# One PSUM pool, half-size weight tiles, and the seven-product form in four of eight pairs of k-tiles

## The chip, the cores and the metric

The kernel runs on one core of one Trainium2 chip. The metric is the time of the whole program on the device, in microseconds (us). Five engines with instruction streams of their own take part: TensorE (PE in the views; PEld is its weight load), VectorE (DVE), ScalarE (ACT), GpSimd (POOL) and SyncE (SP), which here only issues transfers. An engine runs its stream strictly in order; an instruction that has to wait for another engine or for a transfer holds up all that stand behind it on its own engine.

## What is computed

A transformer block on 256 tokens of width 2048: three token mixers run beside each other on the normalised input, their results are merged by gates and projected, and a SwiGLU layer follows. Cut to its large products:

```python
h = rms_norm(x, g_mix)
proj = h @ w_in                                # 2048 -> q/k/v of the mixers and 3 x 2048 gates
...                                            # attention of the mixers gives oa, ob, oc
merged = gate0 * (oa @ w_br_a) + gate1 * (ob @ w_br_b) + gate2 * (oc @ w_br_c)
x = x + merged @ w_o                           # 2048 x 2048
hf = rms_norm(x, g_ffn) @ w_ffn_in             # 2048 -> 2 x 5632
x = x + (silu(hf[:, :5632]) * hf[:, 5632:]) @ w_ffn_out
```

Everything is fp32. Weights are read once, so each goes through the core as it comes from memory.

## The kernel before

**Precision.** A product of fp32 numbers is made of three products of reduced-width numbers. `split` (line 83) writes `hi`, a rounded copy of a tile, by ScalarE (line 86) and `lo = source - hi` by VectorE (line 87). Each product then takes three matmuls into one PSUM bank: hi x hi, hi x lo, lo x hi (lines 183 to 185, or 548 to 550 in the FFN).

**Tiles.** The 256 tokens are two tiles of 128 rows (`T` = 2), the 2048 input channels 16 k-tiles of 128, and outputs come in blocks of 512 columns, one PSUM bank each. `product` (line 161) makes one block of 512 columns for both token tiles. It loads weights through `load` (line 150) in tiles `raw` of 4 k-tiles (1 MB, three buffers), and splits them two k-tiles at a time into `whi` and `wlo` (four buffers each, so a tile takes over the buffer of the tile four before it; `raw` tiles turn in the same way). Weight loads are issued by SP.

**Stages.** In order: keys and values of the memory tokens; the input projection, with the attention work as side jobs between its steps (`tick`, line 140); gates and branch products with the merge (lines 456 to 479); the output projection with the residual and the transposes of the new `x` (lines 482 to 495); the FFN (from line 502).

**FFN.** The 5632 hidden columns are 11 chunks of 512; each chunk takes 512 columns of the half under Silu (A) and the same 512 of the other half (B). `in_seven` (line 525) computes a chunk. It sees two neighbouring k-tiles, the two token tiles and A, B as a 2 x 2 by 2 x 2 block product. In 5 of the 8 pairs of k-tiles it makes the eight block products plainly (steps `d3` to `d7`: 24 matmuls each). In the other three (`s0` to `s2`) it makes seven products (21 matmuls) from sums of blocks: the sums of activations are made once (`stationary_forms`, tiles `fh`, `fl`), the sums of weights by VectorE for each chunk (lines 583, 584, 588, 589; `t2`, `t3`, `t4` hold them), and the steps `6`, `7` and `4` at the end of the list run over the sums of all three. `ORDER` lists the steps of a chunk. The results stand in six banks `mmX`, `mmY`, `mmZ`, `mmW`, `mmV`, `mmQ`; X is copied out twice while it is still summing. At the end of a chunk ScalarE and VectorE combine the banks in `SA` and `SB` (lines 609 to 614), ScalarE takes Silu (623), VectorE multiplies (624), and TensorE transposes the result with the identity (line 229, tiles `tp`) for the second FFN product, which runs after chunks 4, 8 and 11 over the chunks made since. `r_f`, the scale of the second norm for each token, is applied in Silu and in the multiply.

**PSUM.** There are eight banks. Up to the output projection four belong to a pool "mm" (accumulators) and four to a pool "at" (transposes, attention); ahead of the FFN both are closed and opened again with seven and one (lines 503 to 505). The transposes of a chunk thus share one bank.

**Order.** The instruction streams are laid down when the program is built: a scheduler puts each engine's ready instructions in the order of its own estimate of time, with the order of the program text as priority and buffers as limits. What an engine executes next is therefore fixed; which instructions stand beside each other on an engine can only be read from the streams.

Of the kernel before, what the change touches and what calls it, by code (L numbers as in the profile page):

```python
# [18 lines left out]
P = 128  # L19
# [6 lines left out]
NC = 512  # L26
KF = DFF // P
PK, LOAD = 2, 4
# [23 lines left out]
SEVEN = 3  # L52
ORDER = "s0 d3 s1 d4 s2 d5 6 d6 7 d7 4".split()
ORDER0 = "d3 d4 d5 s0 s1 d6 s2 6 d7 7 4".split()
# [3 lines left out]
def encoder_block(ctx: ExitStack, tc: tile.TileContext, a: dict, out: bass.AP):  # L58
# [7 lines left out]
    banks = ExitStack()  # L66
    pools = {"mm": banks.enter_context(tc.tile_pool(name="pmm", bufs=4, space=bass.MemoryType.PSUM)),
             "at": banks.enter_context(tc.tile_pool(name="pat", bufs=4, space=bass.MemoryType.PSUM))}
# [7 lines left out]
    def at_bank(name):  # L76
        return pools["at"].tile([P, NC], F32, name=name, tag="at")

    def mm_bank(name="mm"):
        return pools["mm"].tile([P, NC], F32, name=name, tag="mm")  # L80
# [69 lines left out]
    def load(src, k0, nk):  # L150

        raw = wp.tile([P, LOAD, NC], F32, name="raw")
        if nk % PK:
            c = k0 % PK * NC
            nc.sync.dma_start(out=raw[:, 0], in_=src[k0 // PK][:, c:c + NC])
        else:
            nc.sync.dma_start(out=raw[:, :nk].rearrange("p (u k) n -> p u (k n)", k=PK),
                              in_=src[k0 // PK:(k0 + nk) // PK].rearrange("u p n -> p u n"))
        return raw

    def product(src, lhs, nk, head=(), beside={}):


        ps = [mm_bank() for _ in range(T)]
        k0 = 0
        while k0 < nk:
            n = head[0] if head else min(LOAD, nk - k0)
# [5 lines left out]
            for b in range(0, n, PK):  # L173
                m = min(PK, n - b)
                hi = wp.tile([P, PK, NC], F32R, name="whi", bufs=4)
                lo = wp.tile([P, PK, NC], F32R, name="wlo", bufs=4)
                split(hi[:, :m], lo[:, :m], raw[:, b:b + m])
                for i in range(m):
                    k = k0 + b + i
                    xh, xl = lhs(k)  # L180
                    for t in range(T):
                        c = slice(t * P, (t + 1) * P)
                        nc.tensor.matmul(ps[t], lhsT=xh[:, c], rhs=hi[:, i], start=(k == 0), stop=False)  # L183
# [182 lines left out]
    def attend(qs, ks, vs, bias, kt):  # L366
# [36 lines left out]
        def turn(i):  # L403
# [7 lines left out]
            pTs.append(pT)  # L411

        turn(0)
        ops = at_bank("o")
        for i in range(g):
            yield PV_LAG
            if i + 1 < g:
# [301 lines left out]
```

## Time and profile before

| | |
|---|---|
| median of three timed runs | 1429.48 us (1427.87 to 1429.51) |
| profiled execution | 1432.02 us |
| its span, first to last instruction | 1430.2 us |
| mean granted TensorE clock | 0.994 |
| moved by DMA | 276.99 MB, mean 194 GB/s |

The profiled execution is 2.5 us above the median, and 1.8 us of it lie outside the span. In the rows below, a busy time stands with its share of the span and, after an x, with a count; a group's row gives line, engine, operation, result <- operands, then total busy time and mean nanoseconds of one, then the idle time of that engine just before these instructions with what ended most of it. Matmuls overlap in TensorE's pipeline, so the mean of one (393 ns for `mm<-whi,xT`) is more than the spacing from one to the next. VectorE's splits of weights (`wlo<-raw,whi`, 497 of them) are its largest group with 612.6 us; ScalarE's copies for them (`whi<-raw`) take 524.0 us.

### The profile page before, as it was taken

Reading aid. Unit: us, or ns where it says so; the run is one execution under the profiler, and the core shown is the slowest. Engines: PE = TensorE matmul, PEld = TensorE weight load, DVE = VectorE, ACT = ScalarE, POOL = GpSimd, SP = SyncE. Lnnn points to the kernel's source line nnn. Section 1 sums busy time; section 2 is a strip of 40 time slices with the busy share of each in tenths; the row PEclk is TensorE's granted clock in tenths of the full one; section 3 lists DMA queues with packets and bytes.
Section 4 is the critical chain, followed back from the end, with each engine's and each line's share of the span. In section 5 each row is a group of like instructions: output and inputs, shape, how many; then the busy total and the mean of one; then the engine's idle time right before and its main releaser. Section 6 shows DMA issues by size and latency. Waiting matters only on the chain.

```text
span 1430.2 us, 16503 instructions
## 1 busy us (share of the span) xinstructions
PE 1400.4 (98%) x6323; PEld 1151.6 (81%) x6323; DVE 963.3 (67%) x1191; ACT 741.0 (52%) x971; POOL 78.8 (6%) x146
## 2 busy tenths in 40 slices
PE   6999999999999999999899999999999999999998
PEld 4778788888888888888687788888888888888887
DVE  5666776754455555555688987557988855788763
ACT  5576556544444444444456555435655643456542
POOL 0012642200000000000000000000000000000000
PEclk8999999999999999999999999999999999999999
DMA  8876445456555555655455554555554555655562
GB/s 293 272 255 187 147 175 176 135 218 217 195 180 202 191 169 188 213 181 179 174 177 180 211 186 188 187 195 206 201 186 176 203 206 190 222 176 178 206 223 101
DMA packets 64510, 276.99 MB, mean 194 GB/s; under 512 B 5232, under 2 KB 7792, under 8 KB 52912
## 3 DMA queue, kind: packets, MB, share of 16 engines
q1 hardware_dynamic: 61984, 271.73, 54.8%
q10 hardware_dynamic: 2448, 4.22, 0.9%
q8 instruction: 49, 0.80, 0.2%
q14 instruction: 29, 0.24, 0.0%
HBM read 273.05 MB, written 2.88 MB: 193 GB/s over the span
## 4 chain that ended last, share of the span: by engine, by line
PE 89%; DMA 4%; POOL 2%; DVE 2%; ACT 2%; issue 1%; SPq 0%; ACTq 0%; DVEq 0%; POOLq 0%
PE mm L184 18%; PE mm L183 18%; PE mm L185 18%; PE mmY L549 2%; PE mmY L550 2%; PE mmY L548 2%; PE mmZ L549 2%; PE mmZ L550 2%; PE mmZ L548 2%; PE mmV L549 2%; PE mmV L550 2%; PE mmV L548 2%; PE mmQ L550 2%; PE mmQ L549 2%; PE mmQ L548 2%; PE mmX L549 1%
## 5 line engine op out<-in xcount | busy, mean ns | idle before, releaser
L87 DVE TENSOR_TENSOR wlo<-raw,whi 128x1024 fp32r<-128x1024 f32 (+1 forms) x497 | 612.6, 1238 | 393.4 <-ACT whi L86 392.1
L86 ACT ACTIVATE whi<-raw 128x1024 fp32r<-128x1024 f32 (+1 forms) x497 | 524.0, 1061 | 573.5 <-PE mm L185 367.1
L183 PE MATMUL mm<-whi,xT 128*128 128x512 f32 x640 | 250.6, 393 | 1.4 <-ACT whi L86 1.1
L184 PE MATMUL mm<-wlo,xT 128*128 128x512 f32 x640 | 250.2, 391 | 1.1 <-DVE wlo L87 1.1
L185 PE MATMUL mm<-whi,xT 128*128 128x512 f32 x640 | 249.5, 391 | 0.0
L183 PEld LDWEIGHTS mm<-whi,xT 128*128 128x128 f32 x640 | 120.1, 188 | 26.7 <-ACT whi L86 1.6
L184 PEld LDWEIGHTS mm<-wlo,xT 128*128 128x128 f32 x640 | 120.2, 188 | 26.3 <-DVE wlo L87 1.5
L185 PEld LDWEIGHTS mm<-whi,xT 128*128 128x128 f32 x640 | 120.2, 188 | 24.6
L184 PE MATMUL mm<-wlo,hT 128*128 128x512 f32 x352 | 138.0, 393 | 0.0
L185 PE MATMUL mm<-whi,hT 128*128 128x512 f32 x352 | 137.6, 393 | 0.0
L183 PE MATMUL mm<-whi,hT 128*128 128x512 f32 x352 | 134.9, 391 | 0.0
L184 PEld LDWEIGHTS mm<-wlo,hT 128*128 128x128 f32 x352 | 66.1, 188 | 14.8
L183 PEld LDWEIGHTS mm<-whi,hT 128*128 128x128 f32 x352 | 66.1, 188 | 14.6
L185 PEld LDWEIGHTS mm<-whi,hT 128*128 128x128 f32 x352 | 66.1, 188 | 13.6
L87 DVE TENSOR_TENSOR wlo<-t,whi 128x1024 fp32r<-128x1024 f32 x66 | 62.9, 955 | 6.3 <-ACT whi L86 3.6
L548 PE MATMUL mmY<-whi,x1T 128*128 128x512 f32 x143 | 57.7, 403 | 5.6 <-DVE rs_h L96 5.6
L86 ACT ACTIVATE whi<-t 128x1024 fp32r<-128x1024 f32 x66 | 55.6, 843 | 10.9 <-PE mmX L550 5.7
L549 PE MATMUL mmY<-wlo,x1T 128*128 128x512 f32 x143 | 56.7, 397 | 0.1
L550 PE MATMUL mmY<-whi,x1T 128*128 128x512 f32 x143 | 56.3, 393 | 0.0
L548 PE MATMUL mmV<-whi,x1T 128*128 128x512 f32 x143 | 56.2, 393 | 0.0
L549 PE MATMUL mmV<-wlo,x1T 128*128 128x512 f32 x143 | 55.9, 391 | 0.0
L550 PE MATMUL mmV<-whi,x1T 128*128 128x512 f32 x143 | 55.9, 391 | 0.0
(192 smaller groups left out, 2117.5 us busy)
## 6 DMA issues: line engine op xcount, KB each, us to landing
raw<-in_w_ffn SPq DMA_DIRECT2D x88, 1024.0 KB, 4.9
raw<-in_w_gate SPq DMA_DIRECT2D x48, 1024.0 KB, 5.0
raw<-in_w_ffn_out SPq DMA_DIRECT2D x44, 1024.0 KB, 5.0
raw<-in_w_qkv SPq DMA_DIRECT2D x32, 1024.0 KB, 5.0
raw<-in_w_o SPq DMA_DIRECT2D x16, 1024.0 KB, 4.9
raw<-in_w_br SPq DMA_DIRECT2D x8, 1024.0 KB, 5.0
raw<-in_w_mem SPq DMA_DIRECT2D x15, 512.0 KB, 4.7
raw<-in_w_br SPq DMA_DIRECT2D x8, 512.0 KB, 3.5
```

Source lines behind the costliest of these rows:

```text
L86: nc.scalar.activation(hi, src, AF.Copy)
L87: nc.vector.tensor_sub(lo, src, hi.bitcast(F32))
L183: nc.tensor.matmul(ps[t], lhsT=xh[:, c], rhs=hi[:, i], start=(k == 0), stop=False)
L184: nc.tensor.matmul(ps[t], lhsT=xh[:, c], rhs=lo[:, i], start=False, stop=False)
L185: nc.tensor.matmul(ps[t], lhsT=xl[:, c], rhs=hi[:, i], start=False, stop=(k == nk - 1))
L548: nc.tensor.matmul(ps[b], lhsT=st[0], rhs=hi, start=first, stop=False, skip_group_check=chain)
L549: nc.tensor.matmul(ps[b], lhsT=st[0], rhs=lo, start=False, stop=False, skip_group_check=chain)
L550: nc.tensor.matmul(ps[b], lhsT=st[1], rhs=hi, start=False, stop=stop, skip_group_check=chain)
```

## The change

One PSUM pool of eight banks, `bank`, takes the place of the two; it isn't reopened ahead of the FFN, and products, transposes and attention share it. A `raw` tile holds two k-tiles (512 KB) in place of four, with six buffers in place of three, everywhere; so each weight load of 1 MB becomes two. In the FFN four pairs of k-tiles (`s0` to `s3`) take the seven-product form and four (`d4` to `d7`) the plain one. For that the host lays A and B of a pair of k-tiles in two blocks behind each other (`_pairs`), a pair's step loads them into two tiles `b1` (A) and `b2` (B), and for each `s` step GpSimd issues a DMA that reads the first k-tile of A from memory once more and adds it into the first half of `b2` (256 KB, `accum_op=ALU.add`). VectorE still makes `t2` and `t3` (in the new function `sums`), and the sum for V goes into the second half of `b1` and is split and multiplied within its own step; step `4` and `t4` are gone. The second norm's scale leaves the multiply (line 624 before, 611 now, one operation over both token tiles) and is applied when the second FFN product is taken out of PSUM (line 623 now). Lines with - are of the kernel before.

```diff
-SEVEN = 3
-ORDER = "s0 d3 s1 d4 s2 d5 6 d6 7 d7 4".split()
-ORDER0 = "d3 d4 d5 s0 s1 d6 s2 6 d7 7 4".split()
+SEVEN = 4
+ORDER = "s0 d4 s1 d5 s2 s3 d6 6 d7 7".split()
+ORDER0 = "d4 d5 d6 s0 s1 s2 s3 6 d7 7".split()
...
-    pools = {"mm": banks.enter_context(tc.tile_pool(name="pmm", bufs=4, space=bass.MemoryType.PSUM)),
-             "at": banks.enter_context(tc.tile_pool(name="pat", bufs=4, space=bass.MemoryType.PSUM))}
+    psum = ctx.enter_context(tc.tile_pool(name="psum", bufs=8, space=bass.MemoryType.PSUM))
...
+    def bank(name):
+        return psum.tile([P, NC], F32, name=name, tag="bank")
...
     def load(src, k0, nk):
-        raw = wp.tile([P, LOAD, NC], F32, name="raw")
...
+        raw = wp.tile([P, PK, NC], F32, name="raw", bufs=6)
+        c = k0 % PK * NC
+        nc.sync.dma_start(out=raw[:, :nk].rearrange("p k n -> p (k n)"), in_=src[k0 // PK][:, c:c + nk * NC])
         return raw
...
-    banks.close()
-    pools["mm"] = ctx.enter_context(tc.tile_pool(name="pm2", bufs=7, space=bass.MemoryType.PSUM))
-    pools["at"] = ctx.enter_context(tc.tile_pool(name="pa2", bufs=1, space=bass.MemoryType.PSUM))
...
-                raw = wp.tile([P, LOAD, NC], F32, name="raw")
-                nc.sync.dma_start(out=raw.rearrange("p k n -> p (k n)"), in_=src[u])
+                raws = [load(src, 2 * (2 * u + c), PK) for c in range(2)]
+                if o[0] == "s":
+                    nc.gpsimd.dma_start(out=raws[1][:, 0], in_=src[2 * u][:, :NC], accum_op=ALU.add)
...
             elif o[0] == "s":
-                hi, lo = halves()
-                split(hi, lo, raw[:, :2])
+                b1, b2 = raws
+                hi, lo = halves(b1)
                 mul("X", at(2 * u, 0), hi[:, 0], lo[:, 0])
                 mul("Y", at(2 * u + 1, 0), hi[:, 1], lo[:, 1])
-                hi, lo = halves()
-                nc.vector.tensor_add(t3[:, u], raw[:, 2], raw[:, 3])
-                nc.vector.tensor_add(raw[:, 2], raw[:, 2], raw[:, 0])
-                split(hi, lo, raw[:, 2:])
+                sums(b1, b2, t2[:, u], t3[:, u])
+                hi, lo = halves(b2)
                 mul("W", forms(u, 0), hi[:, 0], lo[:, 0])
                 mul("Z", forms(u, 2), hi[:, 1], lo[:, 1])
-                nc.vector.tensor_add(t2[:, u], raw[:, 2], raw[:, 3])
-                nc.vector.tensor_add(t4[:, u], t2[:, u], raw[:, 1])
                 tick()
+                nc.vector.tensor_add(b1[:, 1], t2[:, u], b1[:, 1])
+                hi, lo = halves(b1[:, 1])
+                mul("V", at(2 * u + 1, 1), hi[:, 0], lo[:, 0])
...
-        nc.vector.tensor_sub(SB[:, 0], SB[:, 0], SA[:, 1])
-        nc.vector.tensor_sub(SA[:, 1], SA[:, 1], SB[:, 1])
         nc.vector.tensor_add(SA[:, 0], ps["Y"], SA[:, 0])
-        nc.vector.tensor_add(SB[:, 1], ps["V"], SB[:, 1])
+        nc.vector.tensor_sub(SB[:, 0], SB[:, 0], SB[:, 1])
         nc.vector.tensor_sub(SB[:, 0], ps["Z"], SB[:, 0])
-        nc.vector.tensor_add(SA[:, 1], ps["Q"], SA[:, 1])
+        nc.vector.tensor_sub(SB[:, 1], SB[:, 1], SA[:, 1])
+        nc.vector.tensor_add(SB[:, 1], ps["Q"], SB[:, 1])
+        nc.vector.tensor_add(SA[:, 1], ps["V"], SA[:, 1])
+        return SA, SB
+
+    def sums(b1, b2, t2, t3):
+        nc.vector.tensor_add(t2, b2[:, 0], b2[:, 1])
+        nc.vector.tensor_sub(t3, t2, b1[:, 0])
...
-                nc.vector.scalar_tensor_tensor(av[t], bv[t], r_f[:, 0, t:t + 1], av[t],
-                                               op0=ALU.mult, op1=ALU.mult)
+            nc.vector.tensor_mul(av, av, bv)
...
+def _pairs(v, w):
+    return np.stack([v, w], 2).reshape(v.shape[0], -1, *v.shape[2:])
...
-        "w_ffn": np.concatenate([_blocks(f[:, :DFF]), _blocks(f[:, DFF:])], -1),
+        "w_ffn": _pairs(_blocks(f[:, :DFF]), _blocks(f[:, DFF:])),
```

In the new kernel the line numbers are: 82 VectorE's half of a split, 218 the transposes, 532 to 534 the three matmuls of the FFN's input product, 557 the adding DMA, 575 the sum for V, 591 to 596 the combination of the banks, 601 and 602 `sums`, 611 the multiply.

**The end of a chunk on TensorE.** The two pieces are from the turn of one chunk to the next in the middle of the FFN. `tp` are the banks of the chunk's transposes, which read `SA` (in the kernel before, `SB` too); X has the highest number where a new chunk begins. In the kernel before, the old chunk's last matmuls are those of `mmV_6507`, and the new chunk opens with `mmX_6813`:

```order
L548 MATMUL mmV_6507<-whi_6770,x1T_5092 128x512
L549 MATMUL mmV_6507<-wlo_6771,x1T_5092 128x512
L550 MATMUL mmV_6507<-whi_6770,x1T_5092 128x512
L548 MATMUL mmX_6813<-whi_6809,x1T_5091 128x512
L548 MATMUL mmY_6817<-whi_6809,x1T_5091 128x512
L549 MATMUL mmX_6813<-wlo_6810,x1T_5091 128x512
L550 MATMUL mmX_6813<-whi_6809,x1T_5091 128x512
L549 MATMUL mmY_6817<-wlo_6810,x1T_5091 128x512
L550 MATMUL mmY_6817<-whi_6809,x1T_5091 128x512
L548 MATMUL mmW_6827<-whi_6821,fh_5773 128x512
L548 MATMUL mmZ_6831<-whi_6821,fh_5773 128x512
L548 MATMUL mmY_6817<-whi_6839,x1T_5092 128x512
```

```order
L548 MATMUL mmV_6846<-whi_6839,x1T_5092 128x512
L229 MATMUL tp_6788<-ident_80,SA_6463 128x128
L548 MATMUL mmQ_6863<-whi_6856,x1T_5092 128x512
L549 MATMUL mmW_6827<-wlo_6822,fh_5773 128x512
L550 MATMUL mmW_6827<-whi_6821,fl_5774 128x512
```

In the new kernel, at the turn from `mmX_6719` to `mmX_7081` (`x4` stands for four transposes behind each other):

```order
L532 MATMUL mmX_6719<-whi_7033,fh_5970 128x512
L533 MATMUL mmX_6719<-wlo_7034,fh_5970 128x512
L534 MATMUL mmX_6719<-whi_7033,fl_5971 128x512
L218 MATMUL tp_7054<-ident_77,SA_6706 128x128 x4
L218 MATMUL tp_7061<-ident_77,SA_6706 128x128 x4
L532 MATMUL mmX_7081<-whi_7077,x1T_5264 128x512
L533 MATMUL mmX_7081<-wlo_7078,x1T_5264 128x512
L534 MATMUL mmX_7081<-whi_7077,x1T_5264 128x512
L532 MATMUL mmY_7085<-whi_7077,x1T_5264 128x512
L533 MATMUL mmY_7085<-wlo_7078,x1T_5264 128x512
L534 MATMUL mmY_7085<-whi_7077,x1T_5264 128x512
L532 MATMUL mmW_7095<-whi_7091,fh_5970 128x512
```

The first transpose stood ten matmuls into the next chunk, and single ones alternated with its matmuls; now all eight stand between the last matmul of one chunk and the first of the next.

**The same turn on VectorE.** Before, from the first sum for the next chunk to the last multiply of the old one, `L624` is the multiply and `L583`, `L584`, `L588`, `L589` are sums of weights for the next chunk:

```order
L583 TENSOR_TENSOR t3_6805<-raw_6873 128x512
L613 TENSOR_TENSOR SB_6464<-mmZ_6492,SB_6464 128x512
L614 TENSOR_TENSOR SA_6463<-mmQ_6524,SA_6463 128x512
L584 TENSOR_TENSOR raw_6873<-raw_6873 128x512
L624 SCALAR_TENSOR_TENSOR SA_6463<-SB_6464,scales_94,SA_6463 128x512
L87 TENSOR_TENSOR wlo_6822<-raw_6807,whi_6821 128x1024
L612 TENSOR_TENSOR SB_6464<-mmV_6507,SB_6464 128x512
L87 TENSOR_TENSOR wlo_6840<-raw_6837,whi_6839 128x1024
L588 TENSOR_TENSOR t2_6804<-raw_6873 128x512
L87 TENSOR_TENSOR wlo_6857<-raw_6837,whi_6856 128x1024
L87 TENSOR_TENSOR wlo_6876<-raw_6873,whi_6875 128x1024
L624 SCALAR_TENSOR_TENSOR SB_6464<-SA_6463,scales_94,SB_6464 128x512
```

In the new kernel, `t2_7070`, `t3_7071` and `raw_7072` to `raw_7151` belong to the next chunk, `SA_6706` and `SB_6707` to the old one. The adding DMA writes to `raw_7074` (step `s0`) and `raw_7151` (`s1`). With six buffers, `raw_7072` and `raw_7074` take over from the tiles of the old chunk's `s3`, the last of which `whi_6921` is made from, and `raw_7151` takes over from `raw_6989`, which `wlo_7008` reads:

```order
L82 TENSOR_TENSOR wlo_6992<-raw_6987,whi_6991 128x1024
L601 TENSOR_TENSOR t2_7070<-raw_7074 128x512
L602 TENSOR_TENSOR t3_7071<-t2_7070,raw_7072 128x512
L82 TENSOR_TENSOR wlo_7008<-raw_6989,whi_7007 128x1024
L82 TENSOR_TENSOR wlo_7024<-t3_6709,whi_7023 128x1024
L592 TENSOR_TENSOR SB_6707<-SB_6707 128x512
L82 TENSOR_TENSOR wlo_7034<-t3_6709,whi_7033 128x1024
L591 TENSOR_TENSOR SA_6706<-mmY_6723,SA_6706 128x512
L82 TENSOR_TENSOR wlo_7078<-raw_7072,whi_7077 128x1024
L593 TENSOR_TENSOR SB_6707<-mmZ_6737,SB_6707 128x512
L575 TENSOR_TENSOR raw_7072<-t2_7070,raw_7072 128x512
L601 TENSOR_TENSOR t2_7070<-raw_7151 128x512
```

```order
L82 TENSOR_TENSOR wlo_7092<-raw_7074,whi_7091 128x1024
L602 TENSOR_TENSOR t3_7071<-t2_7070,raw_7149 128x512
L82 TENSOR_TENSOR wlo_7105<-raw_7072,whi_7104 128x512
L594 TENSOR_TENSOR SB_6707<-SB_6707,SA_6706 128x512
L82 TENSOR_TENSOR wlo_7117<-raw_7112,whi_7116 128x1024
L595 TENSOR_TENSOR SB_6707<-mmQ_6777,SB_6707 128x512
L596 TENSOR_TENSOR SA_6706<-mmV_6746,SA_6706 128x512
L611 TENSOR_TENSOR SA_6706<-SA_6706,SB_6707 128x1024
```

The multiply (`L611`) that the transposes read stands behind both pairs of `sums` of the next chunk and four of its splits. Further on in a chunk, right after the transposes' copies, the stream goes on like this (one chunk earlier; `raw_6860` is the tile of step `s2` to which the DMA adds, its buffer is that of `raw_6752`, and `raw_6822` and `raw_6824` are the tiles of `d5`):

```order
L82 TENSOR_TENSOR wlo_6771<-raw_6752,whi_6770 128x1024
L82 TENSOR_TENSOR wlo_6793<-raw_6787,whi_6792 128x1024
L82 TENSOR_TENSOR wlo_6805<-raw_6789,whi_6804 128x1024
L575 TENSOR_TENSOR raw_6787<-t2_6708,raw_6787 128x512
L82 TENSOR_TENSOR wlo_6816<-raw_6787,whi_6815 128x512
L601 TENSOR_TENSOR t2_6708<-raw_6860 128x512
L602 TENSOR_TENSOR t3_6709<-t2_6708,raw_6858 128x512
L82 TENSOR_TENSOR wlo_6827<-raw_6822,whi_6826 128x1024
L82 TENSOR_TENSOR wlo_6843<-raw_6824,whi_6842 128x1024
```

**Ahead of the FFN on TensorE.** `mm` with `mT` is the output projection, `tp<-...x0, x1` are the transposes of the new `x` for the last 512 columns, and `mmY`, `mmV`, `mmZ`, `mmQ` are the FFN's first chunk. Before:

```order
L185 MATMUL mm_5580<-whi_5701,mT_4234 128x512
L229 MATMUL tp_5722<-ident_80,x0_5087 128x128
L229 MATMUL tp_5731<-ident_80,x0_5087 128x128
L229 MATMUL tp_5722<-ident_80,x1_5088 128x128
L229 MATMUL tp_5722<-ident_80,x0_5087 128x128
L229 MATMUL tp_5722<-ident_80,x1_5088 128x128
L229 MATMUL tp_5731<-ident_80,x1_5088 128x128
L229 MATMUL tp_5731<-ident_80,x0_5087 128x128
L229 MATMUL tp_5731<-ident_80,x1_5088 128x128
L548 MATMUL mmY_5796<-whi_5792,x1T_5092 128x512
L549 MATMUL mmY_5796<-wlo_5793,x1T_5092 128x512
```

In the new kernel two of these transposes come first, then 20 matmuls of the first chunk, of which the last eight are shown here, and then the other six:

```order
L532 MATMUL mmZ_6012<-whi_6008,x1T_5266 128x512
L533 MATMUL mmZ_6012<-wlo_6009,x1T_5266 128x512
L534 MATMUL mmZ_6012<-whi_6008,x1T_5266 128x512
L532 MATMUL mmQ_6016<-whi_6008,x1T_5266 128x512
L533 MATMUL mmQ_6016<-wlo_6009,x1T_5266 128x512
L534 MATMUL mmQ_6016<-whi_6008,x1T_5266 128x512
L532 MATMUL mmZ_6012<-whi_6008,x1T_5266 128x512
L533 MATMUL mmZ_6012<-wlo_6009,x1T_5266 128x512
L218 MATMUL tp_5927<-ident_77,x1_5261 128x128
L218 MATMUL tp_5927<-ident_77,x0_5260 128x128
L218 MATMUL tp_5927<-ident_77,x1_5261 128x128
```

Transposes of `x` stood directly behind each other and ahead of the first `mmY`; now most of the first pair's matmuls stand between them.

103 lines of the change are left out of this document (43 added, 60 removed).

## Prediction

> **What bounds the kernel now.** I read the page's engine line first, then the chain that ended last, then who waits for whom, and last the stretches where the change acts.
>
> ```profile
> span 1430.2 us, 16503 instructions
> PE 1400.4 (98%) x6323; PEld 1151.6 (81%) x6323; DVE 963.3 (67%) x1191; ACT 741.0 (52%) x971; POOL 78.8 (6%) x146
> ...
> PE 89%; DMA 4%; POOL 2%; DVE 2%; ACT 2%; issue 1%; SPq 0%; ACTq 0%; DVEq 0%; POOLq 0%
> ```
>
> TensorE is busy for 98% of the span and carries 89% of the chain: the time is the number of matmuls times their spacing, plus the places where TensorE stands still. The next rows give the spacing and the largest of those places.
>
> ```profile
> core 0: us, PE busy (x) PEld busy (x) DVE busy (x) ACT busy (x) POOL busy (x), PEclk, DMA share, GB/s
> 400.00:500.00 100.00, 100.00 (x443) 82.81 (x442) 54.20 (x53) 44.28 (x45) 0.00 (x0) 1.00 0.56 192
> 711.00:716.00 5.00, 4.82 (x13) 3.89 (x14) 4.66 (x15) 1.48 (x1) 0.00 (x0) 0.56 0.00 0
> 1017.00:1147.00 130.00, 129.94 (x584) 106.60 (x583) 113.17 (x130) 78.41 (x93) 0.00 (x0) 1.00 0.56 197
> ```
> ```profile
> PE mm L183 <- ACT memT L89: 13.4, 3, 7.0
> ...
> PE mmY L548 <- DVE rs_h L96: 5.6, 1, 5.6
> ```
> ```profile
> L229 PE MATMUL tp<-ident,SA 128*128 128x128 f32 x44 | 11.4, 272 | 0.2 <-DVE SA L624 0.2
> ```
>
> From 400 to 500 us a matmul goes out every 100.00/443 = 0.226 us. TensorE waits 13.4 us for the first activations and 5.6 us ahead of the FFN. Inside the FFN input product (1017 to 1147 us are three chunks) it never stands, though VectorE is 113.17/130 = 87% busy there. The last row matters most: the transposes at a chunk's end wait 0.2 us in all, since TensorE works on the next chunk while VectorE and ScalarE finish the last one.
>
> **Fewer matmuls.** A chunk goes from 3x21 + 5x24 = 183 matmuls to 4x21 + 4x24 = 180; the built streams differ by the same 33 (6320 and 6287). 33 x 0.226 = **-7.4 us**.
>
> **Front of the FFN.** The new stream has ready matmuls there instead of transposes followed by a wait, so the 5.6 us go, and so does the slow clock behind them: from 711 to 716 us the granted clock was 0.56 and 13 matmuls took 5.00 us where 13 x 0.226 = 2.94 us would do, 2.1 us lost. A larger `fraw` (512 for 384 columns) is late next; I leave 0.7 us. **-7.0 us**.
>
> **Chunk ends.** Here the order decides. Before, one transpose bank came free twice and the transposes stood among the next chunk's matmuls. Now all eight stand directly behind the chunk's last `mmX`, ahead of every matmul of the next chunk, in all 11 chunks. They read `SA` after the multiply of line 611, and that needs the last `mmX`. TensorE must therefore wait out the whole epilogue, 11 times. Its length, from rows of VectorE and ScalarE at a chunk end of before:
>
> ```profile
> 844.75 0.68 DVE L612 TENSOR_TENSOR SB<-mmV,SB 128x512 f32<-128x512 f32 x1
> 845.35 1.22 DVE L87 TENSOR_TENSOR wlo<-raw,whi 128x1024 fp32r<-128x1024 f32 x1
> 846.48 0.69 DVE L588 TENSOR_TENSOR t<-raw 128x512 f32<-128x512 f32 x1
> ```
> ```profile
> 845.47 0.73 ACT L623 ACTIVATE SB<-SB,scales 128x512 f32<-128x512 f32 x1 [0.23 <-DVE SB L612]
> ```
> ```profile
> L86 ACT ACTIVATE whi<-raw 128x1024 fp32r<-128x1024 f32 (+1 forms) x497 | 524.0, 1061 | 573.5 <-PE mm L185 367.1
> L86 ACT ACTIVATE hT<-tp 128x512 fp32r<-128x512 f32 x22 | 12.9, 588 | 2.8 <-PE tp L229 2.8
> ```
>
> On VectorE a 512-column operation follows the one before it after 0.60 us (844.75 to 845.35) and a 1024-column one takes 1.13 us of the queue (845.35 to 846.48); finished they are after 0.68 and 1.22. Shortest way from the end T of the last matmul: a matmul's end trails its spacing by 0.2; ScalarE's copy of X 0.59, its next weight split 1.06, VectorE's half of that split (`wlo_7117`, queued ahead) 1.13, line 595 0.60, line 596 0.68, Silu 0.73, multiply 1.22: **6.2 us**. That is the price where a group of chunks ends and no accumulating DMA stands in the way: 3 x 6.2 = **+18.6 us**.
>
> At the other 8 ends VectorE's stream also holds the sums of the next chunk, and two of them wait for the accumulating DMA. Call its time from issue to landing A. No row of before shows one. The nearest rows, by bytes and queue:
>
> ```profile
> raw<-in_w_gate SPq DMA_DIRECT2D x48, 1024.0 KB, 5.0
> ...
> raw<-in_w_br SPq DMA_DIRECT2D x8, 512.0 KB, 3.5
> rawT<-in_memT ACTq DMA_DIRECT2D x8, 256.0 KB, 4.6
> ...
> rawT<-in_xT ACTq DMA_DIRECT2D x8, 256.0 KB, 5.0
> ...
> out<-x SPq DMA_DIRECT2D x6, 256.0 KB, 2.4
> ...
> gh<-in_g_heads SPq DMA_DIRECT2D x1, 384.0 KB, 10.0
> ```
>
> 256 KB take 2.4 us with the queues empty and 4.6 to 5.0 beside other loads; 384 KB behind a full queue took 10.0. I bound A by 2.4 and 10.0 and take **A = 5.0**, the row with the same bytes beside weight loads. The Trainium skill ("DMA: Bandwidth & Descriptors", the section on the anatomy of a DMA on the gpsimd path) fits such a DMA as about 2.0 us plus bytes at 436 GB/s, an estimate of 2.6 us for 256 KB. By that the sum would be the quick rival's below.
>
> Now the chain. The split `whi_6921` takes the buffer of `whi_6875`, free 90 matmuls (20.3 us) before T; its two halves end about T-19 and free the last buffer that the next chunk's first two half tiles need. Their 1 MB lands 5.0 later, T-14, and the first sum can run at T-14+A. Two sums and `wlo_7008` (0.60+0.60+1.13) free the buffer of `raw_7151`; its load takes 3.5, its accumulating DMA A again: T-8.2+2A. Behind it stand, in order, a sum, a split, a sum, a half split, line 594, a split, lines 595, 596, Silu and multiply: 0.60+1.13+0.60+0.60+0.60+1.13+0.60+0.68+0.73+1.22 = 7.9. So the transposes start at T+2A-0.3, and with some 0.3 us of semaphore hops TensorE stands for about 2A = 10.0 us, never under 6.2. 8 x 10.0 = **+80.0 us**.
>
> After each of these 11 stops the clock is low again, as at 711 us after 5.6 us of idling: 11 x 2.1 = **+23.1 us**. The skill ("TensorE: Matmul & The Clock Gate", Part 1) puts the low state at half clock until one busy window of about 3.4 us is over, an estimate of 1.7 us a stop, 18.7 in all; the trace's 2.1 is the measured one and is used.
>
> **Waits inside a chunk.** VectorE's sum for `s2` stands ahead of the splits of `d5`. Its buffer comes free by the split `wlo_6771`, 6 slow matmuls (2.6 us) plus 1.06 + 1.13 after the chunk starts, 4.8; plus 3.5, plus A, plus two sums and a split 2.33: 10.6+A. TensorE needs that split after 54 matmuls, 12.2 + 2.1 slow + 0.4 for two that go first: 14.7. So A-4.1 = 0.9 us, 8 chunks: **+7 us**. The three chunks that open a group come without the lead that a stop gives; in the first, three sums for `s0` to `s2` precede the split that `s0` ends on. Between 0 and 9 us each, 4 taken: **+12 us**.
>
> **The one PSUM pool elsewhere.** At the four merge steps the first transpose now stands directly behind the branch product and waits for one multiply and one addition (2 x 0.68, and hops): 1.5 us each, **+6 us**. At the start two pairs of `memT` splits now stand behind weight splits that wait for TensorE: 2 x (1.06 + 0.6), **+3 us**, with the 13.4 us of waits there as the scale of what a new order may win or lose (I allow -5 to +10). Half-size loads themselves cost SP a second issue and are hidden, as DMA has 44% to spare (share 0.56); 44 accumulations add 11.5 MB to 277.
>
> **VectorE as the bound?** A chunk now holds about 21 operations of 1024 and 24 of 512 columns: 21 x 1.13 + 24 x 0.60 = 38.1 us for 180 x 0.226 = 40.7 of TensorE. Near, but not over, and the stops give it time.
>
> **The sum.** The profiled execution took 1432.0 us, span and 1.8 around it. 1432.0 - 7.4 - 7.0 + 18.6 + 80.0 + 23.1 + 7 + 12 + 6 + 3 = 1567.3. The median of the timed runs lies 2.5 below that execution (1429.5): **1565 us**, slower by 9.5%.
>
> **Rivals.**
> - *The accumulation is quick.* At A = 2.4 to 3 every end costs the least, 6.2: 11 x (6.2 + 2.1) = 91, no wait inside but 3 for the first chunks, 9 for pool and start, less 14.4: 1432.0 + 89 - 2.5 = 1518 us. For it: the 2.4 us row, and the skill's 2.6. Against it: weight loads run beside, GpSimd has to prepare the transfer, and the target is read as well as written.
> - *The accumulation is slow.* At A = 8: 8 x 16 + 18.6 + 23.1 + 8 x 4 + 3 x 8 + 9 - 14.4 = 220: 1650 us; at 10 about 1700. For it: the 10.0 us row, and that reading, adding and writing may take more than a copy.
> - *Not slower.* The epilogue stays covered, as today's 0.2 us in 44 transposes; then only 33 matmuls and the FFN's front are left: 1432.0 - 14.4 + 9 - 2.5 = 1424 us. It decides once a chunk end costs under (14.4 - 9)/11 = 0.5 us, clock included. Against it: the multiply that the transposes read needs a copy, an addition, Silu and itself behind the last matmul, 3.2 us with nothing between them.
>
> **How the numbers follow.** Forecast (A from 3.2 to 7): 0.60. Quick: 0.20. Slow: 0.15. Not slower: 0.05. The range takes in the quick case with a few us of luck at the start, 1510, and the slow one to A about 9, 1675; the not-slower case and the slowest end stay out. The chances count 0.2% as no change, about what a measurement of this kernel can tell: slower 0.95, same 0.01, faster 0.04.
>
> **What would show it.** In the changed kernel's profile the transposes of `SA` (line 218) should have over 80 us of idle time before them, released by VectorE's multiply (line 611), 6 us at the group ends and about 10 at the others; the clock row should fall below 0.7 behind each; the sums of line 601 should wait on `raw` DMAs; the issue rows should show the 256 KB accumulation landing about 5 us after issue; the wait ahead of the first `mmY` should be gone. The forecast is wrong if those transposes wait under 1 us, or if the accumulation lands outside 3 to 7 us.

## The result, and the profile after

The changed kernel takes 1640.97 us (median of four runs, 1639.30 to 1647.61) against 1429.33 us: ratio 1.149, 95% interval 1.146 to 1.153. Its profiled execution, the slowest of the four, took 1647.61 us with a span of 1645.8, which is 215.6 us more than the span before; the working below is made against these spans. From the page of the changed kernel, the span, the engines, and the granted clock in 40 slices:

```profile
span 1645.8 us, 17399 instructions
PE 1456.7 (89%) x6290; PEld 1179.5 (72%) x6290; DVE 989.0 (60%) x1202; ACT 761.9 (46%) x993; POOL 116.6 (7%) x190
...
PEclk7999999999999999998889899997897999888999
```

TensorE fell from 98% to 89% of its span, with 33 matmuls fewer. Apart from the first slice, its clock falls below 0.9 in the second half only, which is the FFN. Busy time by stretch of the changed kernel (the stretch in us, then each engine's busy us and count, the clock, the DMA share, GB/s): a steady stretch, the stop at one chunk's end and the 5 us behind it, a wait inside the next chunk and the 5 us behind it, and the whole FFN:

```profile
core 0: us, PE busy (x) PEld busy (x) DVE busy (x) ACT busy (x) POOL busy (x), PEclk, DMA share, GB/s
400.00:500.00 100.00, 100.00 (x443) 82.81 (x442) 51.83 (x49) 43.03 (x43) 0.00 (x0) 1.00 0.64 195
...
1111.40:1122.20 10.80, 0.00 (x0) 0.00 (x0) 7.61 (x10) 2.78 (x4) 0.00 (x0) 0.72 0.59 166
1122.20:1127.20 5.00, 4.94 (x18) 4.28 (x18) 1.38 (x3) 1.65 (x3) 0.00 (x0) 0.58 0.02 9
1137.90:1141.60 3.70, 0.13 (x1) 0.00 (x0) 2.49 (x4) 1.20 (x2) 0.86 (x1) 0.79 0.28 39
1141.60:1146.60 5.00, 4.92 (x12) 3.86 (x13) 4.96 (x7) 0.20 (x1) 0.00 (x0) 0.50 0.90 243
729.00:1645.00 916.00, 761.77 (x3132) 610.21 (x3131) 568.54 (x633) 398.60 (x447) 38.14 (x44) 0.91 0.56 162
```

The same for the FFN of the kernel before:

```profile
711.20:1430.00 718.80, 713.08 (x3157) 584.87 (x3157) 537.82 (x608) 375.01 (x416) 0.00 (x0) 1.00 0.54 189
```

The FFN takes 916.0 us in place of 718.8, so 197.2 of the loss lie there, and 17.8 ahead of it (729.0 less 711.2). In the FFN TensorE stood still for 916.0 - 761.8 = 154 us (5.7 before; about 4 us of either lie behind the last matmul), and what it did went slower: 761.77/3132 = 0.243 us for a matmul in place of 713.08/3157 = 0.226, over 3132 of them 54 us. Ahead of the FFN the steady stretch is as fast as before: from 400 to 500 us the same 443 matmuls stand. Who waited for whom in the changed kernel (us in total, times, the longest):

```profile
DVE t L601 <- DMA raw<-in_w_ffn: 120.0, 31, 7.7
...
PE tp L218 <- DVE SA L611: 100.7, 11, 11.0
...
PE mmY L533 <- DVE wlo L82: 32.6, 11, 4.0
...
PE mm L172 <- ACT memT L84: 18.0, 4, 9.0
...
PE hT L346 <- POOL y L320: 6.3, 1, 6.3
PE tp L218 <- DVE mg L465: 6.0, 4, 1.5
```

The transposes wait for the multiply of line 611, 11 times, 100.7 us in all. One of these stops on VectorE, GpSimd and TensorE (start, duration, instruction, in brackets the idle time before it and what ended it):

```profile
1103.46 0.69 DVE L601 TENSOR_TENSOR t<-raw 128x512 f32<-128x512 f32 x1 [3.09 <-DMA raw<-in_w_ffn]
1104.19 0.69 DVE L602 TENSOR_TENSOR t<-t,raw 128x512 f32<-128x512 f32 x1
1104.80 1.22 DVE L82 TENSOR_TENSOR wlo<-raw,whi 128x1024 fp32r<-128x1024 f32 x1
...
1114.22 0.69 DVE L601 TENSOR_TENSOR t<-raw 128x512 f32<-128x512 f32 x1 [2.40 <-DMA raw<-in_w_ffn]
1114.83 1.22 DVE L82 TENSOR_TENSOR wlo<-raw,whi 128x1024 fp32r<-128x1024 f32 x1
...
1117.17 0.69 DVE L594 TENSOR_TENSOR SB<-SB,SA 128x512 f32<-128x512 f32 x1
...
1120.98 1.22 DVE L611 TENSOR_TENSOR SA<-SA,SB 128x1024 f32<-128x1024 f32 x1 [0.79 <-ACT SA L610]
```
```profile
1110.18 0.86 POOL L557 DMA_DIRECT2D raw<-in_w_ffn  x1 [11.35 <-DVE SA L591]
```
```profile
1110.96 0.39 PE L534 MATMUL mmX<-whi,fl 128*128 128x512 f32 x1
1122.26 1.97 PE L218 MATMUL tp<-ident,SA 128*128 128x128 f32 x8 [10.91 <-DVE SA L611]
```

The first sum waits for the first landing; the split behind it (1104.80) frees a buffer; its load, issued at 1106.0, lands at 1109.6, GpSimd issues the addition at 1110.18 (the row names line 591, which ended just then, but the addition needs the landed load), and the second sum starts at 1114.22, 3 us after TensorE's last matmul. Line 594, which needs nothing later than the copy of X, stands behind that sum in VectorE's stream, and the multiply ends at 1122.2. The landing times, from the page's issue rows and, last, the least, median and greatest of the 44 additions:

```profile
raw<-in_w_ffn SPq DMA_DIRECT2D x176, 512.0 KB, 4.1
raw<-in_w_gate SPq DMA_DIRECT2D x96, 512.0 KB, 3.6
...
raw<-in_w_ffn POOLq DMA_DIRECT2D x44, 256.0 KB, 4.5
```
```profile
DMA to landing us min/median/max: 3.9/4.5/6.9
```

Taken apart by their place in the chunk, the medians of the additions are 4.8, 4.0, 6.3 and 4.1 us for `s0`, `s1`, `s2` and `s3`.

### The profile page after: what moved, and what is told of

It is laid out like the page before. It is cut to its first block, busy times and chain, and to the rows that moved or that the text cites. A ratio compares the mean times of both kernels' runs of the same rounds, so it can differ in the third digit from the quotient of the medians.

```text
span 1645.8 us, 17399 instructions
## 1 busy us (share of the span) xinstructions
PE 1456.7 (89%) x6290; PEld 1179.5 (72%) x6290; DVE 989.0 (60%) x1202; ACT 761.9 (46%) x993; POOL 116.6 (7%) x190
## 5 line engine op out<-in xcount | busy, mean ns | idle before, releaser
L82 DVE TENSOR_TENSOR wlo<-raw,whi 128x1024 fp32r<-128x1024 f32 (+1 forms) x541 | 639.7, 1193 | 446.1 <-ACT whi L81 444.2
L81 ACT ACTIVATE whi<-raw 128x1024 fp32r<-128x1024 f32 (+1 forms) x541 | 548.5, 1024 | 647.7 <-PE mm L174 400.0
L172 PE MATMUL mm<-whi,hT 128*128 128x512 f32 x352 | 139.9, 397 | 0.0
L174 PE MATMUL mm<-whi,hT 128*128 128x512 f32 x352 | 139.2, 396 | 0.0
L173 PEld LDWEIGHTS mm<-wlo,xT 128*128 128x128 f32 x640 | 120.5, 188 | 23.7
L557 POOL DMA_DIRECT2D raw<-in_w_ffn x44 | 38.1, 867 | 1212.7 <-DMA raw<-in_w_ffn 473.4
L218 PE MATMUL tp<-ident,SA 128*128 128x128 f32 x88 | 21.4, 425 | 100.7 <-DVE SA L611 100.7
L601 DVE TENSOR_TENSOR t<-raw 128x512 f32<-128x512 f32 x44 | 30.2, 690 | 120.0 <-DMA raw<-in_w_ffn 120.0
L218 PEld LDWEIGHTS tp<-ident,SA 128*128 128x128 f32 x88 | 17.3, 224 | 105.1 <-issue 83.5
L532 PE MATMUL mmV<-whi,x1T 128*128 128x512 f32 x132 | 54.6, 413 | 6.9 <-ACT whi L81 6.9
L533 PEld LDWEIGHTS mmY<-wlo,x1T 128*128 128x128 f32 x132 | 28.0, 212 | 43.7 <-DVE wlo L82 37.9
```

The source lines that it names most:

```text
L81: nc.scalar.activation(hi, src, AF.Copy)
L82: nc.vector.tensor_sub(lo, src, hi.bitcast(F32))
L173: nc.tensor.matmul(ps[t], lhsT=xh[:, c], rhs=lo[:, i], start=False, stop=False)
L174: nc.tensor.matmul(ps[t], lhsT=xl[:, c], rhs=hi[:, i], start=False, stop=(k == nk - 1))
L218: nc.tensor.transpose(tp[:, k * S + t * P:k * S + (t + 1) * P], src[t][:, (2 * h + k) * P:(2 * h + k + 1) * P], ident)
L532: nc.tensor.matmul(ps[b], lhsT=st[0], rhs=hi, start=first, stop=False, skip_group_check=chain)
```

## The experiments

The questions were: is it the place of the transposes, the adding DMA, VectorE's load with a fourth pair, or the half-size tiles?

### The sum on VectorE, the order kept

```diff
-                if o[0] == "s":
-                    nc.gpsimd.dma_start(out=raws[1][:, 0], in_=src[2 * u][:, :NC], accum_op=ALU.add)
...
+                nc.vector.tensor_add(b2[:, 0], b2[:, 0], b1[:, 0])
                 sums(b1, b2, t2[:, u], t3[:, u])
```

> The changed kernel with the 44 adding DMAs taken out and the same sum made by VectorE (44 more additions of 512 columns, 0.60 us of its queue each); everything else as changed, and the transposes still stand between the last matmul of a chunk and the first of the next in all 11 chunks. Theory (place and landing together: the transposes wait out the epilogue, and the DMA's landing lengthens it at 8 ends and holds up one sum inside each chunk): the stops shrink to the epilogue alone, 11 x 6.4 us, with 11 x 2.1 us of slow clock; the waits ahead of mmY inside the chunks (34.3 us) and their slow clock go; so 1641 - (103 - 70) - 45 - 25 = about 1540 us. Rival D (the adding DMA alone is to blame, the place of the transposes costs nothing): about 1445 us, and the transposes wait under 10 us in all. Rival V (VectorE is the bound with a fourth seven-product pair): slower still, 1641 + 26 = about 1667 us.

Measured: 1559.78 us, ratio to before 1.091 (1.089 to 1.093), so 81 us less than the changed kernel, and 20 more than was expected. Its waits:

```profile
PE tp L218 <- DVE SA L610: 78.9, 11, 8.0
```

The mean stop is 7.2 us, not 6.4: the three at the ends of groups of chunks are 6.2, the other eight 7.0 to 8.0, with the sums and the extra additions in VectorE's queue ahead of the operation that is line 594 in the changed kernel. The waits ahead of `mmY` are gone. Rivals D and V fall: without an addition to wait for, the transposes still cost most of what they did.

### The two PSUM pools of before, the DMA kept

```diff
-    psum = ctx.enter_context(tc.tile_pool(name="psum", bufs=8, space=bass.MemoryType.PSUM))
+    banks = ExitStack()
+    pools = {"mm": banks.enter_context(tc.tile_pool(name="pmm", bufs=4, space=bass.MemoryType.PSUM)),
+             "at": banks.enter_context(tc.tile_pool(name="pat", bufs=4, space=bass.MemoryType.PSUM))}
...
+    banks.close()
+    pools["mm"] = ctx.enter_context(tc.tile_pool(name="pm2", bufs=7, space=bass.MemoryType.PSUM))
+    pools["at"] = ctx.enter_context(tc.tile_pool(name="pa2", bufs=1, space=bass.MemoryType.PSUM))
```

> The changed kernel with the two PSUM pools of the kernel before (four and four banks, then seven and one), the adding DMA kept. The first transposes of a chunk then stand 49 to 51 matmuls behind the chunk's last one, inside the next chunk. Theory: the stops ahead of the transposes (101 us) and their slow clock (23 us) go, the merges (7 us) and the start (13 us) come back, the wait ahead of the FFN (7 us) returns; the waits of VectorE's sums for the adding DMA stay, and some that lay inside the stops now show: 1500 to 1540 us, transposes waiting under 5 us. Rival D (the DMA alone): 1600 us or more, since VectorE still waits for 44 landings. Rival V (VectorE's load): 1600 us or more, with VectorE over 95% busy in a chunk.

Measured: 1542.06 us, ratio 1.080 (1.077 to 1.083), just above what was expected. The transposes wait for nothing any more. In their place, among TensorE's and VectorE's waits:

```profile
DVE t L608 <- DMA raw<-in_w_ffn: 112.5, 37, 7.2
...
PE mmV L540 <- DVE wlo L85: 21.6, 20, 5.2
...
PE mmW L540 <- DVE wlo L85: 16.8, 7, 3.1
...
PE mmY L540 <- DVE wlo L85: 10.1, 5, 4.9
```

VectorE waits nearly as long for landings as in the changed kernel (112.5 and 120.0 us), and what lay under the stops shows ahead of other matmuls. The two pools are worth 99 us, 7 of them ahead of the FFN, whose first matmul starts at 722.0 us in place of 729.0. The landings have a price of their own.

### Both undone

> The changed kernel with both undone: the two PSUM pools of before, and the sum on VectorE in place of the adding DMA; the half-size tiles and four seven-product pairs stay. Theory: neither stops nor waits for a landing are left; 1430 - 7.4 for 33 matmuls fewer, plus what VectorE's load costs (about 40.5 us of 40.7 in a chunk): 1425 to 1460 us. Rival D: the same as with the sum on VectorE alone, within 10 us of that run. Rival V or a loss by the half-size tiles: over 1490 us.

Measured: 1464.83 us, ratio 1.025 (1.023 to 1.026). The four kernels make a square, in us:

| | adding DMA | sum on VectorE |
|---|---|---|
| one pool, transposes at the chunk's end | 1640.97 | 1559.78 |
| two pools, transposes in the next chunk | 1542.06 | 1464.83 |

The one pool with its place of the transposes costs 98.9 or 95.0 us, the DMA 81.2 or 77.2, nearly independent of each other. But 35 us above the kernel before were left where at most 30 were expected, with 33 matmuls fewer. That part is neither of the two.

### Later in the program text, with one pool

```diff
-            for t in range(T):
-                nc.scalar.activation(av[:, t], av[:, t], AF.Silu, scale=r_f[:, 0, t:t + 1])
-            nc.vector.tensor_mul(av, av, bv)
...
-            transposed([av[:, t] for t in range(T)], lambda k, m: (tl[:, 0, k:k + m], tl[:, 1, k:k + m]))
+            start(turn_over(av, bv, tl))
...
+    def turn_over(av, bv, tl):
+        yield 3
+        ...
```

The side job holds the lines taken out, unchanged.

> The changed kernel, one PSUM pool and adding DMAs kept, with Silu, the multiply and the transposes of a chunk written later in the program text, as a side job that starts three steps into the next chunk; the transposes then stand 46 to 51 matmuls behind the chunk's last one. Theory (it is the place that costs, not the pool as such): like the run with the two pools of before, 1542 us, plus merges and start of the one pool (about +8) less the wait ahead of the FFN (-6): 1535 to 1560 us, transposes waiting under 10 us. Rival (banks of one pool come free too late, whatever the order): over 1600 us.

Measured: 1551.83 us, ratio 1.086 (1.083 to 1.089), within 10 us of the run with two pools and 89 us below the changed kernel, though the pool is the same. The transposes of `SA` wait for nothing. So it is the place in the stream, not the pool as such. It fits that a pool hands out its banks in the order of the program text, in which the transposes' banks stand between those of two chunks; that was read from the built streams and not tried by itself.

### The kernel before with one pool alone

> The kernel before with one PSUM pool of eight banks and nothing else changed. Its first transpose of a chunk then stands directly behind the chunk's last matmul (ten matmuls into the next chunk before), and the others 10 to 40 matmuls further. The epilogue needs less behind the last matmul there: the first multiply does not read V, the bank that ends last. Theory: merges +7 us, start -5 to +15, the wait ahead of the FFN -6, chunk ends 11 x 0.5 to 2 us: 1430 to 1460 us. Rival (one pool by itself brings the stops of the changed kernel, about 6.4 + 2.1 us at each of 11 ends): 1520 us or more.

Measured: 1445.21 us, ratio 1.011 (1.010 to 1.013). Its waits at chunk ends and merges:

```profile
PE tp L227 <- DVE SA L619: 7.2, 7, 1.2
PE tp L227 <- DVE mg L474: 6.0, 4, 1.5
PE hT L355 <- POOL y L329: 2.5, 1, 2.5
```

With the old end of a chunk one pool costs 7 us there, not 101. The merges cost the 6.0 us that were forecast. The input projection starts 3.6 us later (66.3 us in place of 62.6), 2.5 of them in the wait for GpSimd in the last row. In return the wait of 5.6 us ahead of the FFN is gone. What in the new end of a chunk makes the difference, X as the bank that ends last or one multiply over both token tiles, was not tried by itself.

### A plain copy in place of the addition

```diff
-                    nc.gpsimd.dma_start(out=raws[1][:, 0], in_=src[2 * u][:, :NC], accum_op=ALU.add)
+                    nc.gpsimd.dma_start(out=raws[1][:, 0], in_=src[2 * u][:, :NC])
```

> The changed kernel with the 44 DMAs as plain copies: the same 256 KB from the same place into the same half tile, issued by GpSimd, without the addition (so the first k-tile of B is overwritten by that of A and the products of the four pairs are not those of the reference). TensorE, VectorE and ScalarE run the same instructions in the same order. Theory (a stop at a chunk end with sums is the two landings plus about 1.6 us, never under 6.4; the wait inside a chunk is the third landing less what covers it): with a landing time of A in place of the 4.5 us of the addition, each us less takes up to 2 us from 8 ends and 1 us from 11 waits inside. If the addition is what makes it long (A near 3): about 1590 to 1600 us. If it is the issue by GpSimd and the traffic (A above 4): 1625 to 1645 us. Rival (the landing doesn't matter, only the waiting order does): within 3 us of 1641 whatever A is.

This kernel leaves the addition out. Measured: 1602.72 us, ratio 1.122 (1.120 to 1.124). The landing of its 44 copies, and the stops:

```profile
DMA to landing us min/median/max: 2.7/3.4/5.2
```
```profile
PE tp L218 <- DVE SA L611: 90.4, 11, 9.8
```

The addition by itself takes 4.5 - 3.4 = 1.1 us more than the same transfer without it, and 44 times 1.1 us of landing is worth 38 us of the kernel. The rival that the landing doesn't matter falls.

### Each addition twice

```diff
                     nc.gpsimd.dma_start(out=raws[1][:, 0], in_=src[2 * u][:, :NC], accum_op=ALU.add)
+                    nc.gpsimd.dma_start(out=raws[1][:, 0], in_=src[2 * u][:, :NC], accum_op=ALU.add)
```

> The changed kernel with each adding DMA issued twice, one behind the other (so the sum holds A twice and the products of the four pairs are not those of the reference). The second one waits for the first, so a sum waits for about 2 x 4.5 us. Theory: 8 stops longer by the landings of s0 and s1, 4.8 + 4.0 = 8.8 us each (+70), the wait for the third sum longer by 6.3 us in 8 chunks (+50), the chunks that open a group +5 each: 1760 to 1790 us, with the transposes' idle time near 170 us. Rival (the landing is covered by the weight loads, and the stops come from the epilogue alone): under 1670 us.

Measured: 1709.29 us, ratio 1.195 (1.192 to 1.197): 68 us more than the changed kernel, where 120 to 150 were expected, and the transposes wait 106.1 us, not 170. The scheduler laid VectorE's stream out otherwise. At the chunk's end there it reads (in the order of issue):

```
L82 TENSOR_TENSOR wlo_7020<-raw_7001,whi_7019 128x1024
L82 TENSOR_TENSOR wlo_7036<-t3_6717,whi_7035 128x1024
L593 TENSOR_TENSOR SB_6715<-SB_6715 128x512
L602 TENSOR_TENSOR t2_7082<-raw_7086 128x512
```

The split that frees the buffer for `s1` now stands ahead of the first sum (behind it in the changed kernel), so the two landings no longer follow one another: one doubled landing lies in the chain where two single ones lay, and the rest moved into the chunk. TensorE's other waits in the FFN add up to 88 us there, and to 50 in the changed kernel. The doubling does cost, but the run doesn't measure the formula for a stop, and the expectation should have been read off the new stream.

### The kernel before with half-size tiles alone

`load` as in the change, six buffers of two k-tiles; each 1 MB load of the FFN becomes two of 512 KB; the rest stays.

> The kernel before with half-size weight tiles (two k-tiles, 512 KB, six buffers) and nothing else changed; TensorE's order is that of before. Theory: only the start suffers, where small loads queue ahead of the first activations: +8 to +12 us, 1438 to 1442 us, and the FFN is within 3 us of before. Rival (half-size tiles take away lead everywhere, and are behind the 35 us that are left with both undone): 1455 us or more. Rival (hidden altogether): within 3 us of 1430.

Measured: 1453.62 us, ratio 1.017 (1.015 to 1.018), 24 us slower. Its waits, and the stretch from 400 to 500 us, where the kernel before had a DMA share of 0.56 at 192 GB/s:

```profile
DVE t L578 <- DMA raw<-in_w_ffn: 52.0, 27, 3.8
...
PE mm L179 <- ACT memT L89: 17.8, 4, 8.7
```
```profile
400.00:500.00 100.00, 100.00 (x443) 82.84 (x442) 52.08 (x49) 44.23 (x45) 0.00 (x0) 1.00 0.64 194
```

The same bytes keep the DMA engines busy for 14% longer. The FFN's first matmul starts at 721.9 us in place of 711.2, most of it lost at the start, where TensorE waits 17.8 us for activations (13.4 before); and in the FFN VectorE's sums wait 52.0 us for loads (6.0 before). So both the theory's start and the rival's lost lead are true, about half each (10.7 us ahead of the FFN, 12.1 in it). These 24 us explain most of what both undone had left. The remaining 11 us between that run and this one must lie in what else that run keeps of the change, such as the fourth pair with V in its own step and half-width splits; its `mmV` waits 6.3 us for ScalarE and 3.6 for VectorE. This rest was not taken apart further.

### The front of the FFN, and four pairs, in the form of before

The kernel before, its pools swapped one step earlier (first diff); the kernel before with four pairs (second diff); both.

```diff
             nc.scalar.activation(junk[:, t], xc, AF.Square, accum_out=ss1[:, t, n:n + 1])
+        if n == 3:
+            banks.close()
+            pools["mm"] = ctx.enter_context(tc.tile_pool(name="pm2", bufs=7, space=bass.MemoryType.PSUM))
+            pools["at"] = ctx.enter_context(tc.tile_pool(name="pa2", bufs=1, space=bass.MemoryType.PSUM))
         transposed([x[t][:, n * NC:(n + 1) * NC] for t in range(T)],
```

```diff
-SEVEN = 3
-ORDER = "s0 d3 s1 d4 s2 d5 6 d6 7 d7 4".split()
-ORDER0 = "d3 d4 d5 s0 s1 d6 s2 6 d7 7 4".split()
+SEVEN = 4
+ORDER = "s0 d4 s1 d5 s2 d6 s3 6 d7 7 4".split()
+ORDER0 = "d4 d5 d6 s0 s1 s2 s3 6 d7 7 4".split()
```

> The kernel before with its two pools closed and opened again one step earlier: ahead of the last transposes of the new x in place of behind them. The first matmul of the FFN then takes a bank that has long been free, and four of the last eight transposes stand behind it. Theory (the only gain of the changed kernel besides its fewer matmuls is that the FFN's front has work while the last transposes are taken out): the wait of 5.6 us and about 2 us of slow clock go: 1421 to 1424 us, ratio 0.994 to 0.996. Rival (the wait is for the activations, not for a bank, and moves to the next matmul): within 2 us of 1429.

> The kernel before with four seven-product pairs in place of three, in its own form: whole 1 MB tiles, its two PSUM pools, all four sums of a pair made by VectorE, t4 and step 4 kept; 33 matmuls fewer. Theory (the fourth pair by itself is not what costs): -7.4 us for the matmuls, and VectorE, at 87% in a chunk before, goes to about 93% and gives part of it back: 1422 to 1432 us. Rival V (VectorE becomes the bound): 1445 us or more.

> The kernel before with both: the pools swapped ahead of the last transposes, and four seven-product pairs in its own form. Theory: the two add up, 1414 to 1424 us. Rival (the earlier start of the FFN's products takes from VectorE the time that the fourth pair needs): no better than the earlier swap alone.

Measured: the earlier swap 1421.65 us, ratio 0.995 (0.993 to 0.996), faster than both kernels of this study. The wait ahead of the FFN is gone:

```profile
L549 PE MATMUL mmY<-whi,x1T 128*128 128x512 f32 x143 | 57.1, 399 | 0.0
```

Four pairs alone: 1429.13 us, ratio 0.999 (0.998 to 1.000). Both: 1427.87 us, ratio 0.999 (0.998 to 1.000), so they don't add up; where the gain of the earlier swap went there was not taken apart. Three chunks of the kernel with four pairs, and where its matmuls of X wait:

```profile
1012.00:1142.00 130.00, 127.24 (x570) 104.10 (x569) 123.83 (x142) 81.16 (x91) 0.00 (x0) 1.00 0.56 195
```
```profile
L548 PE MATMUL mmX<-whi,x1T 128*128 128x512 f32 x44 | 18.1, 412 | 7.4 <-ACT whi L86 7.3
```

VectorE is busy for 123.83/130 = 95% of a chunk (87% before), and `mmX` waits 7.4 us, as much as 33 matmuls fewer had saved. But these waits are not for VectorE. They are eight of 0.92 us, each at the turn to a new chunk. One of them, on ScalarE and TensorE:

```profile
1012.92 1.06 ACT L86 ACTIVATE whi<-raw 128x1024 fp32r<-128x1024 f32 x1 [0.67 <-PE mmY L550]
```
```profile
1014.03 0.50 PE L548 MATMUL mmX<-whi,x1T 128*128 128x512 f32 x1 [0.92 <-ACT whi L86]
```

TensorE waits for a split of ScalarE, which has itself been idle for 0.67 us until a matmul of `mmY` was done. Of its operands only the `whi` buffer depends on TensorE, so the ring of four `whi` buffers is the likely limit; more buffers were not tried. A fourth pair gains nothing in the form of before.

## Why the prediction came out as it did

The direction, the mechanism and the range held: 1641 us lies between 1510 and 1675, and the transposes are where the largest part went. The forecast of 1565 was 76 us too low (80 by the profiled execution, 1647.6 against 1567.3), and its steps say where: 2 us at the chunk ends, 25 in the slow clock, 31 in the waits inside chunks and 16 ahead of the FFN are 74 of these 80.

- **Chunk ends**: forecast 18.6 + 80.0 = 98.6 us, measured 100.7 in 11 waits. The chain was as worked out, in the order of its rows. The three stops at group ends are 6.2 us each, the sum that was made for them. That the other eight came out so near, 10.3 in the mean against 10.0, is in part luck: the two landings were 4.7 and 4.0 us (medians of these ends) where 5.0 was taken for each, but the first addition was issued 0.7 us later than worked out, and the second 4.2 us behind the split that frees its buffer, not 3.5. With other places of the transposes their wait goes to nothing.
- **Fewer matmuls, merges, FFN front**: 33 fewer (6323 to 6290) and 6.0 us at the merges, as forecast. For the front 7.0 us were forecast: from the last matmul of the output projection to the FFN's first it is 0.9 us in place of 7.7, and the earlier swap alone gives -7.9 us.
- **Slow clock**: forecast 11 x 2.1 = 23.1 us, measured 48. The price of a stop was right, the count was not. From the spacing of the matmuls behind each wait, the 11 ends cost 23.7 us together, and 10 of the waits inside the chunks cost another 24. (The 54 us above also hold the tails of the last matmuls ahead of the waits, each busy for 0.39 us where the next would have started after 0.23; that is some 5 us, and no term of the forecast.) The row from 1141.6 to 1146.6 us shows one wait inside a chunk: after 3.65 us of idling the clock is 0.50 and 12 matmuls take 5 us. The step that failed is "after each of these 11 stops": waits of 2.5 to 4 us can count as well.
- **Waits inside a chunk**: forecast 7 + 12 = 19 us, measured 50 (154 less 100.7 and less the 4 us behind the last matmul): about 27 in the eight chunks, 22 in the three that open a group. The place and the chain were right (the sum for `s2` ahead of the splits of `d5`), the size was not. The third addition lands 6.3 us after its issue, where one value of 5.0 was used for all, its load takes 4.0 in place of 3.5, and the split that frees its buffer ended at 5.2 us, not 4.8. Taken as A - 4.1 = 0.9 us, a difference of near numbers, it came out at 2.4 to 4.0 us.
- **Start**: forecast +3, with -5 to +10 allowed. The 17.8 us that were lost ahead of the FFN already hold the gain of its front. The output projection's last matmul starts at 728.2 us in place of 703.4, 24.7 later, and 6.0 of that are the merges: 18.7 where 3 was forecast. It was put down to the one pool. By the same mark the pool alone is 11.5 us late, merges included, and the half-size tiles alone 10.7. The largest single wait that is new is one of 6.3 us in which transposes of the attention (`hT`) wait for GpSimd; it is 2.5 with the pool alone, and the kernels with two pools have no such wait.
- **Half-size loads "hidden, as DMA has 44% to spare"**: wrong. They cost 24 us in the kernel before, about half of it ahead of the FFN and half in it, where VectorE's waits for loads grew from 6.0 to 52.0 us. A share of free DMA time doesn't tell how long a single load takes, on which a chain with few buffers depends.
- **VectorE as the bound**: "near, but not over" held for the changed kernel, whose stops leave it idle. In the kernel before with four pairs VectorE is 95% busy in a chunk, and TensorE's waits there are still not for it: they stand behind ScalarE's splits at the chunk turns.

Of the rivals, the quick accumulation (1518 us) was refuted by its landings, the slow one (1650) comes near in time for another reason: the landings were 4.5 us in the median, and the time went to the clock and the waits inside. "Not slower" fell with the first wait row.

## What to carry to other kernels

When instructions of a chunk's end are issued by an in-order engine ahead of the next chunk's work, their price is the whole chain behind the last matmul, however small each piece; look at the built stream for what stands between, and move the consumer later in the program text before touching pools. An operation moved from a busy engine to a DMA is not free when its result is needed within a few buffers' time: its landing time counts in every chain that it enters, and a wait that is moved out of one stop shows up in the next. Count a penalty that follows a stop once for every stop, the small ones too: here some waits of 2.5 us already paid it.

## What was not expected of the hardware

- The clock drops after shorter waits than had been thought. In the changed kernel, from 600 us on, the five waits of 1.1 to 1.9 us were followed by 0.1 us of lost time each, those of 2.5 to 3.2 us by 0.1 to 2.5, and every one of 3.3 us and more by 1.6 to 3.0 us (a wait is taken from one matmul's start to the next, less 0.227, which is some 0.2 us more than the idle time in the rows; the loss is worked out from the spacing of the matmuls over the next 7 us). In the trace's record of the granted clock, each low stretch between the FFN's first and last matmul lasts one, two, three or four times 3.41 us. The Trainium skill ("TensorE: Matmul & The Clock Gate", Part 1) describes a free-running window of about 3.4 us in which activity is watched. The lengths of the low stretches agree with it, and so does it that waits of about 3 us cost in one place and not in another; the waits of 2.5 us that cost 1.6 are shorter than one such window.
- A DMA that adds takes 1.1 us more from issue to landing than one that copies the same 256 KB (4.5 and 3.4 us), and holds GpSimd's queue for 0.87 us in place of 0.54.
- Half-size loads with the same bytes raise the DMA share from 0.56 to 0.64 at the same rate, with 79557 packets in place of 64510. The Trainium skill ("Perfetto Trace Analysis", DMA Optimizations) says that splitting DMAs may let a task complete sooner where the DMA engines are generally idle. Here, at a share of 0.56, the split cost 24 us; engines that are busy for more than half the time are not that case, so the run doesn't contradict the page.
